# First sums behind the retention multiplied later, and a third gate tile ahead of the first latent projection

## The chip, the cores and the metric

The kernel runs on one core of one Trainium2 chip. The time is the device time of one execution in microseconds; lower is better. Three runs of the kernel before took 850.65, 853.06 and 853.61 us, median 853.06 us.

## What is computed

Three blocks in a row on x of 256 positions by 1024 channels, all in fp32. The change lies in the first two:

```python
# layer 0, retention: its tail
y = (silu(gate) * group_norm(o)) @ w_out          # 2048 -> 1024
x = x + rms_norm(y, post_norm_g)                  # needs the sum of y*y over the channels
x = x + (p @ ple_w_proj) * sigmoid(x @ ple_w_gate)
# layer 1, latent attention: 16 heads
z = rms_norm(x) @ w_in                            # c_q 768, c_kv 256, k_rope 64, gate 2048
c_q, c_kv = rms_norm(z[:768]), rms_norm(z[768:1024])
q = c_q @ w_uq;  k = c_kv @ w_uk;  v = c_kv @ w_uv
o = softmax(causal(q k^T + q_rope k_rope^T)) v
y = (silu(gate) * o) @ w_out
```

The third block is a convolution block with a feed-forward part, which the change does not touch.

## The kernel before

Channels lie on the partitions, so a tile of a projection is 128 output channels by 256 positions. Every operand is split into a high and a low part, and one product is three matmuls (lines 237 to 239): high by high, high by low, low by high. A call of `mm` does these three. Weights come in loads of 128 by 1024 (eight tiles) through SP's queue; a load is cast to its high part on ScalarE (L178) and subtracted to its low part on VectorE (L179), into five buffers each. Activations are split in the same way by L187 (ScalarE) and L188 (VectorE).

The order of the work is written out by hand with a clock that counts only planned TensorE time: each call of `mm` moves it on by 3 x 256 / 2400 = 0.32 us, and `after(us, fn)` puts `fn` at the first call that ends at or past the due time. On top of that the Tile framework puts the instructions of each engine into a list: earlier in the program goes first, but what its own estimate takes as not ready is passed by what is. The engines then work through their lists in that order.

**The tail of the retention.** `out_proj` runs the output projection: eight blocks m of 128 channels, for each the last four of sixteen input blocks (four calls, twelve matmuls). When the block pairs (0,1), (2,3), (4,5) end, `done` gives them to `Sums.feed`: squares on ScalarE (L327) and their running sum on VectorE (L331). Blocks 6 and 7 come singly. `Sums.flush` takes a PSUM bank, starts the reciprocal root's function on ScalarE with one element (`warm`, L317) and multiplies the running sum by a matrix of ones (L341, two fp32 matmuls, each shown as two); `Sums.end` squares a single block (L357) and adds its product with ones. `flush` falls due 1.0 after block 5, the end of block 6 falls due 1.28 after block 6, and `done(7)` ends the rest. Then `post` takes the reciprocal root, scales and adds (L379 to L381, L367 to L373, L690, L691), splits, and runs the gate projection `ple_gate0`; between them stands `ple_proj` (tiles php), which needs none of this.

**The latent attention.** After the six tiles of c_q, `lora` falls due 4.0 later: sum, reciprocal root, scaling (L792) and split (L187, L188) of the six tiles `lat` that all of `mla_proj` needs. The loop over p (eight pairs of heads) is quoted by the program below. `mla_gate(n)` is sixteen calls of `mm` into two banks, a scaling on VectorE (L831) and a Silu on ScalarE (L832). `mla_proj(p)` is 26 calls: 6 for the rotary part of q, 12 for the rest of q, 4 for k, 4 for v; rotary part and splits follow on ScalarE (L756, L187, copies) and VectorE (L758 to L760, L188). `mla_scores(p)` falls due 3.07 after a projection; it is followed by the softmax (VectorE L896 to L909, ScalarE exponentials L901 and L902), 7.6 later by `mla_turn` (transposes, L920, and splits) and 2.59 after that by `mla_av`. With the list `[2, 4, 6, 8, ...]` two gate tiles stand ahead of each of the first four projections and none ahead of the last four. A step of the modulation for the third block (L413, `ada`, with a DMA) is put in every 7.61 of the planned clock.

Of the kernel before, what the change touches and what calls it, by code (L numbers as in the profile page):

```python
# [82 lines left out]
def tile_kernel(ctx, tc, order, xT, pT, pos, vec, cst, cv, rows, wada, wts, outT):  # L83
# [56 lines left out]
    def small(n):  # L140
        return sp.tile([P, n], F32, tag="small", name=nm("sm"), bufs=8)
# [61 lines left out]
    def after(us, fn):  # L203
        queue.append((clk[0] + us, fn))
        queue.sort(key=lambda e: e[0])
# [4 lines left out]
    def mod_rate(us):  # L210
        mods["rate"], mods["last"] = us, clk[0]
# [13 lines left out]
    def drain():  # L225
        busy[0] = True
        while queue:
            due, fn = queue.pop(0)
            clk[0] = max(clk[0], due)
            fn()  # L230
        busy[0] = False
# [425 lines left out]
    def proj_sums(both, get, key):  # L657

        sums = Sums(both, 0)

        def done(m, ys):
            x = get(m, ys)
            if m < 6:
                sums.feed(x)
                if m == 5:
                    after({"r": 1.0, "m": 0.96}[key], sums.flush)
            elif m == 6:
                after({"r": 1.28, "m": 1.06}[key], lambda: sums.end(x, False))
            else:
                drain()  # L670
                sums.end(x, True)
        return sums, done
# [66 lines left out]
    sums, done = proj_sums(False, lambda m, ys: ys.piece(m), "r")  # L739
# [82 lines left out]
    def mla_gate(p):  # L822

        if p % 2 == 0:
            sgs[p // 2] = Blk(4)
        ps = bank2()
        for b in range(2):
            for kb in range(8):
                mm(ps[:, b, :], seq_g.next(), rhs(xp, kb), kb == 0, kb == 7)
        gr = t2()  # L830
        V.scalar_tensor_tensor(gr, ps, -0.5, bc2(r1["nr"]), MUL, MUL)  # L831
        A.activation(sgs[p // 2].pair(p % 2), gr, AF.Silu)  # L832
# [12 lines left out]
    def mla_proj(p):  # L845
        st = hd[p]
        psr = bank()[:, :S]
        for kb in range(6):
            mm(psr, seq_q.next(), lat_rhs(kb), kb == 0, kb == 5)
        qr = st["qr"] = (t1(F32R, "qrh", 2), t1(F32R, "qrl", 2))  # L850
        rope4(psr, lambda a: split(qr[0], qr[1], a))
        psq = bank2()
        for b in range(2):
            for kb in range(6):
                mm(psq[:, b, :], seq_q.next(), lat_rhs(kb), kb == 0, kb == 5)

        qk0 = st["qk0"] = t2().rearrange("p x (b t) -> p x b t", b=2)
        qp = t2(F32R).rearrange("p x (b t) -> p x b t", b=2)
        qn = st["qn"] = [qp[:, i] for i in range(2)]
        split(*qn, psq[:, :, P:])  # L860
        A.copy(qk0[:, 0], psq[:, :, :P])
        psk = bank2()
        for b in range(2):
            for kb in range(2):
                mm(psk[:, b, :], seq_k.next(), lat_rhs(kb, 6), kb == 0, kb == 1)
        kn = st["kn"] = (t2(F32R), t2(F32R))
        split(kn[0], kn[1], psk)
        A.copy(qk0[:, 1], psk[:, :, :P])
        psv = bank2()
        ws = [seq_v.next() for _ in range(2)]  # L870
        for b in range(2):
            bs = slice(b * P, (b + 1) * P)
            for kb in range(2):
                c = lat_rhs(kb, 6)
                mm(psv[:, b, :], (c[0][:, bs], c[1][:, bs]), ws[kb], kb == 0, kb == 1)
        v = st["v"] = t2(F32R), t1()
        split(v[0][:, 0, :], v[0][:, 1, :], psv[:, 0, :])
        A.copy(v[1], psv[:, 1, :])

    def mla_scores(p):  # L880
        st = hd[p]
        qn, kn, qr, qk0 = st["qn"], st["kn"], st["qr"], st["qk0"]
        st["p"] = []

        ps0 = bank()[:, :S].rearrange("p (e t) -> p e t", e=2)
        mm(ps0, (qr[0][:, :P], qr[1][:, :P]), (kr[0][:, :, :P], kr[1][:, :, :P]), True, False)
        ps1 = bank2()
        mm(ps1, (qr[0][:, P:], qr[1][:, P:]), kr, True, False)
        for e in range(2):
            mm32(ps0[:, e, :], qk0[:, 0, e, :], qk0[:, 1, e, :], False, e == 1)  # L890
        for e in range(2):
            mm(ps1[:, e, :], (qn[0][:, e, :], qn[1][:, e, :]), (kn[0][:, e, :], kn[1][:, e, :]), False, e == 1)
        for e in range(2):
            sm = tp.tile([P, 384], F32, tag="am", name=nm("sm"), bufs=2)
            mx = small(2)
            V.tensor_tensor_reduce(sm[:, :P], ps0[:, e, :], causal[:, P:], 1.0, NEG, ADD, ALU.max, mx[:, 0:1])  # L896
            V.tensor_tensor_reduce(sm[:, P:], ps1[:, e, :], causal, 1.0, NEG, ADD, ALU.max, mx[:, 1:2])
            ngm = small(2)
            V.tensor_scalar(ngm, mx, -1.0, None, MUL)
            ssum = small(2)  # L900
            A.activation(sm[:, :P], sm[:, :P], AF.Exp, bias=ngm[:, 0:1], accum_out=ssum[:, 0:1])  # L901
            A.activation(sm[:, P:], sm[:, P:], AF.Exp, bias=ngm[:, 1:2], accum_out=ssum[:, 1:2])  # L902
            rin = small(2)
            V.reciprocal(rin, ssum)
            for i, part in enumerate((sm[:, :P], sm[:, P:])):
                if 0 >> (2 * (p > 3) + i) & 1:
                    A.activation(part, part, AF.Copy, scale=rin[:, i:i + 1])
                else:
                    V.tensor_scalar(part, part, rin[:, i:i + 1], None, MUL)  # L909
            st["p"].append(sm)  # L910
        after(7.6, lambda: mla_turn(p))
# [30 lines left out]
    mod_rate(7.61)  # L942
    ng = 0
    for p in range(8):
        while ng < [2, 4, 6, 8, 8, 8, 8, 8][p]:
            mla_gate(ng)
            ng += 1
        if p == 4:
            mod_rate(12.84)
        mla_proj(p)  # L950
        after(3.07, lambda p=p: mla_scores(p))

    sums, done = proj_sums(False, lambda m, ys: ys.piece(m), "m")
# [446 lines left out]
    for tb in range(2):  # L1400
# [19 lines left out]
        sq, r = small(1), small(1)  # L1420
# [86 lines left out]
```

## Time and profile before

| | |
|---|---|
| median of 3 runs | 853.06 us (850.65 to 853.61) |
| the profiled execution | 847.85 us, of which the span of instructions is 846.1 us |
| TensorE (PE) busy | 826.1 us, 98% of the span, 6114 matmuls |
| VectorE (DVE) busy | 703.1 us, 83% |
| ScalarE (ACT) busy | 555.2 us, 66% |
| granted TensorE clock | 0.997 of full speed, mean |

Busy times overlap. A matmul of 256 columns is shown with some 0.28 us, but a new one starts about every 0.12 us, so PE's busy time is the time in which at least one is under way. In the rows, the time in square brackets is the idle time of the engine just before an instruction, and behind the arrow stands what ended it.

### The profile page before, as it was taken

What the parts mean: (1) busy time and instruction counts of PE and PEld (TensorE: products, weight loads), DVE (VectorE), ACT (ScalarE), POOL (GpSimd) and SP (SyncE); (2) the same over time, 40 slices, a digit from 0 to 9 for tenths busy, and PEclk for the clock granted to TensorE, in tenths of its full rate; (3) what the DMA queues carried; (4) which work ended last, traced back from release to release, by engine and by line L of the source; (5) the groups of instructions that cost most, each with busy time, mean ns of one, the idle gap of its engine ahead of it and who ended that gap; (6) DMA issues with size and microseconds to landing.
All of it is one profiled execution on the core that took longest, in us unless ns stands there. A gap on an engine that the chain in (4) does not pass through costs nothing.

```text
span 846.1 us, 15771 instructions
## 1 busy us (share of the span) xinstructions
PE 826.1 (98%) x6114; PEld 787.9 (93%) x6114; DVE 703.1 (83%) x1283; ACT 555.2 (66%) x968; POOL 9.9 (1%) x30
## 2 busy tenths in 40 slices
PE   8999999999999999998999999999999999999995
PEld 6989999999999989998999999999998999999885
DVE  6999798988889978688874768899677888889986
ACT  7655565545676686777754857999756576666550
POOL 0000000000000000000000000000000000000001
PEclk9999999999999999999999999999999999999998
DMA  9875567778556637374255364245463455567722
GB/s 335 323 258 212 215 217 269 255 264 319 171 182 248 223 145 259 116 263 145 99 184 176 121 224 152 98 150 199 148 224 128 134 190 191 184 214 255 277 77 75
DMA packets 46634, 167.48 MB, mean 198 GB/s; under 512 B 5216, under 2 KB 5472, under 8 KB 46560
## 3 DMA queue, kind: packets, MB, share of 16 engines
q1 hardware_dynamic: 45936, 164.38, 55.1%
q0 software_dynamic: 624, 2.10, 0.9%
q8 instruction: 48, 0.79, 0.4%
q14 instruction: 26, 0.21, 0.1%
HBM read 165.41 MB, written 1.05 MB: 197 GB/s over the span
## 4 chain that ended last, share of the span: by engine, by line
PE 50%; DVE 2%; ACT 1%; issue 1%; DVEq 0%
PE ps L238 13%; PE ps L237 13%; PE ps L239 13%; PE ps L243 10%; PE ps L341 1%; PE ps L363 0%; DVE wl L179 0%; PE ps L920 0%; PE ps L1170 0%; DVE t L1434 0%; DVE sm L1415 0%; DVE half L690 0%; DVE t L1411 0%; DVE t L1412 0%; PE ps L1407 0%
## 5 line engine op out<-in xcount | busy, mean ns | idle before, releaser
L237 PE MATMUL ps<-half,wh 128*128 128x256 f32 x1504 | 425.4, 284 | 1.4 <-ACT half L187 1.4
L238 PE MATMUL ps<-half,wh 128*128 128x256 f32 x1504 | 423.8, 282 | 0.6 <-DVE half L188 0.5
L239 PE MATMUL ps<-half,wl 128*128 128x256 f32 x1504 | 422.0, 281 | 1.1 <-DVE wl L179 1.0
L178 ACT CAST wh<-raw 128x1024 fp32r<-128x1024 f32 x233 | 243.5, 1049 | 154.9 <-PE ps L238 94.8
L179 DVE TENSOR_TENSOR wl<-raw,wh 128x1024 fp32r<-128x1024 f32 x233 | 282.7, 1219 | 59.5 <-ACT wh L178 57.3
L239 PEld LDWEIGHTS ps<-half,wl 128*128 128x128 f32 x1504 | 283.8, 189 | 1.7 <-DVE wl L179 1.7
L238 PEld LDWEIGHTS ps<-half,wh 128*128 128x128 f32 x1504 | 283.4, 188 | 1.9 <-DVE half L188 1.0
L237 PEld LDWEIGHTS ps<-half,wh 128*128 128x128 f32 x1504 | 282.5, 188 | 2.6 <-ACT half L187 2.0
L243 PE MATMUL ps<-half,raw 128*128 128x256 f32 (+2 forms) x384 | 84.9, 380 | 0.0
L243 PEld LDWEIGHTS ps<-half,raw 128*128 128x128 f32 x384 | 72.5, 190 | 10.0
L237 PE MATMUL ps<-wh,half 128*128 128x512 f32 (+1 forms) x202 | 72.6, 360 | 0.9 <-ACT wh L178 0.9
L413 DVE CUSTOM_DVE_ANT_0 adach<-adach,siluc 128x1024 f32<-128x1024 f32 x48 | 58.4, 1218 | 16.7 <-DMA adach<-in_wada 16.7
L238 PE MATMUL ps<-wl,half 128*128 128x512 f32 (+1 forms) x202 | 71.0, 351 | 0.5 <-DVE wl L179 0.5
L239 PE MATMUL ps<-wh,half 128*128 128x512 f32 (+1 forms) x202 | 71.0, 352 | 0.0
L1087 ACT ACTIVATE t<-apad,vec 128x256 f32<-128x256 f32 x106 | 44.3, 501 | 0.5 <-DVE half L1088 0.5
L237 PEld LDWEIGHTS ps<-wh,half 128*128 128x128 f32 x202 | 37.9, 188 | 6.8 <-ACT wh L178 1.7
L238 PEld LDWEIGHTS ps<-wl,half 128*128 128x128 f32 x202 | 38.1, 189 | 6.0 <-DVE wl L179 1.0
L239 PEld LDWEIGHTS ps<-wh,half 128*128 128x128 f32 x202 | 38.0, 188 | 5.6
L1088 DVE TENSOR_TENSOR half<-half,t 128x512 f32<-128x512 f32 x53 | 36.5, 689 | 3.7 <-ACT t L1087 1.8
L187 ACT CAST half<-t 128x256 fp32r<-128x256 f32 (+1 forms) x47 | 20.3, 453 | 17.9 <-DVE t L1347 10.9
L188 DVE TENSOR_TENSOR half<-t,half 128x256 fp32r<-128x256 f32 (+1 forms) x47 | 21.7, 482 | 4.5 <-ACT half L187 3.6
L1342 ACT ACTIVATE t<-ps,vec 128x256 f32<-128x256 f32 x38 | 21.0, 558 | 2.0 <-PE ps L239 1.2
(290 smaller groups left out, 908.1 us busy)
## 6 DMA issues: line engine op xcount, KB each, us to landing
raw<-in_wts SPq DMA_DIRECT2D x257, 512.0 KB, 4.1
adach<-in_wada SPq DMA_DIRECT2D x48, 512.0 KB, 5.0
half<-in_xT SPq DMA_DIRECT2D x4, 256.0 KB, 5.7
half<-in_rows POOLq DMA_DIRECT2D x2, 512.0 KB, 4.7
out<-t SPq DMA_DIRECT2D x4, 256.0 KB, 2.0
cst<-in_cst SPq DMA_DIRECT2D x1, 928.0 KB, 10.6
raw<-in_wts SPq DMA_DIRECT2D x2, 256.0 KB, 4.4
siluc<-in_cv SPq DMA_DIRECT2D x1, 512.0 KB, 9.0
```

What stands on the lines that cost most here:

```text
L178: A.copy(hi, raw)
L179: V.tensor_sub(lo, raw, hi.bitcast(F32))
L187: A.copy(hi, src)
L188: V.tensor_sub(lo, src, hi.bitcast(F32))
L237: T.matmul(ps, l[0], r[0], start=first, stop=False)
L238: T.matmul(ps, l[0], r[1], start=False, stop=False)
L239: T.matmul(ps, l[1], r[0], start=False, stop=last)
L243: T.matmul(ps, w, r, start=first, stop=last)
L413: V.tensor_tensor_reduce(ch, ch, sc, 1.0, 0.0, MUL, ADD, mod[:, n:n + 1])
L1087: A.activation(t[:, b, :], apad[:, i0 + b, k:k + S], AF.Copy, scale=w[b])
L1088: V.tensor_add(acc.pair(i0 // 2), acc.pair(i0 // 2), t)
L1342: A.activation(t[:, b, :], ps[:, b, :], AF.Identity, bias=col("b_dw_f_2", m), scale=w[2])
```

## The change

Two numbers. The first sums behind the retention fall due 2.0 instead of 1.0 of the planned clock after block 5. The list of gate tiles begins with 3 instead of 2: gate tile 2 is called ahead of `mla_proj(0)` and not behind it, so that one tile (3) instead of two stands between the first and the second projection. All else is as it was; nothing is computed more or less.

```diff
@@ proj_sums, done
                 if m == 5:
-                    after({"r": 1.0, "m": 0.96}[key], sums.flush)
+                    after({"r": 2.0, "m": 0.96}[key], sums.flush)
@@ the loop over the pairs of heads
     for p in range(8):
-        while ng < [2, 4, 6, 8, 8, 8, 8, 8][p]:
+        while ng < [3, 4, 6, 8, 8, 8, 8, 8][p]:
             mla_gate(ng)
             ng += 1
```

## Rows read from the trace of the kernel before

**Rows 1.** The page, part 1: busy us, share of the span, instructions of each engine.

```profile
PE 826.1 (98%) x6114; PEld 787.9 (93%) x6114; DVE 703.1 (83%) x1283; ACT 555.2 (66%) x968; POOL 9.9 (1%) x30
```

**Rows 2.** Windows: stretch, length; busy us (instructions) of PE, PEld, DVE, ACT, POOL; clock; DMA.

```profile
207.00:218.00 11.00, 9.65 (x72) 9.06 (x72) 9.20 (x18) 7.96 (x17) 0.00 (x0) 1.00 0.61 207
264.00:280.20 16.20, 14.83 (x125) 14.57 (x124) 15.53 (x29) 8.28 (x12) 0.00 (x0) 1.00 0.73 259
280.20:293.10 12.90, 12.90 (x108) 12.90 (x109) 12.09 (x25) 9.89 (x20) 0.00 (x0) 1.00 0.55 192
293.10:312.00 18.90, 17.47 (x140) 16.60 (x139) 13.82 (x33) 16.10 (x30) 0.00 (x0) 1.00 0.38 138
...
363.00:390.00 27.00, 25.95 (x213) 25.28 (x213) 22.78 (x59) 19.98 (x44) 0.20 (x1) 1.00 0.61 210
390.00:404.00 14.00, 12.25 (x101) 11.95 (x101) 12.91 (x34) 11.18 (x33) 0.00 (x0) 1.00 0.47 164
```

**Rows 3.** Timelines of ACT, DVE and PE at the tail of the retention: start, length, instruction.

```profile
207.18 0.38 ACT L357 ACTIVATE t<-ps 128x256 f32<-128x256 f32 x1
...
207.41 1.22 DVE L179 TENSOR_TENSOR wl<-raw,wh 128x1024 fp32r<-128x1024 f32 x1
208.55 0.68 DVE L331 TENSOR_TENSOR t<-t,t 128x512 f32<-128x512 f32 x1
...
209.37 1.53 PE L341 MATMUL ps<-t,ones 128*128 128x256 f32 x6 [1.09 <-DVE t L331]
...
217.58 0.39 PE L238 MATMUL ps<-half,wh 128*128 128x256 f32 x1 [0.26 <-DVE half L188]
```

**Rows 4.** Timeline of PE where the first latent projection begins.

```profile
280.19 0.62 PE L237 MATMUL ps<-half,wh 128*128 128x256 f32 x3 [1.37 <-ACT half L187]
```

**Rows 5.** Timeline of DVE around the same place.

```profile
277.67 1.22 DVE L179 TENSOR_TENSOR wl<-raw,wh 128x1024 fp32r<-128x1024 f32 x1
278.80 1.65 DVE L792 SCALAR_TENSOR_TENSOR t<-ps,gq,t 128x256 f32<-128x256 f32 x4
280.37 1.42 DVE L188 TENSOR_TENSOR half<-t,half 128x256 fp32r<-128x256 f32 x4
...
283.09 1.22 DVE L179 TENSOR_TENSOR wl<-raw,wh 128x1024 fp32r<-128x1024 f32 x1
284.23 0.75 DVE L188 TENSOR_TENSOR half<-t,half 128x256 fp32r<-128x256 f32 x2
```

**Rows 6.** Timeline of PE from the first scores to the second projection.

```profile
294.15 0.61 PE L243 MATMUL ps<-t 128*128 128x128 f32 x4
...
303.38 0.70 PE L920 MATMUL ps<-ident,sm 128*128 128x128 f32 x3 [0.45 <-DVE sm L909]
...
305.06 0.39 PE L239 MATMUL ps<-half,wl 128*128 128x256 f32 x1 [0.73 <-DVE wl L179]
...
308.40 0.39 PE L239 MATMUL ps<-half,wl 128*128 128x256 f32 x1 [0.24 <-DVE wl L179]
```

**Rows 7.** Timeline of ACT in the same stretch, and its first Silu table.

```profile
281.08 1.28 ACT L832 ACT_TABLE_LOAD   x1
...
298.59 1.28 ACT L832 ACT_TABLE_LOAD   x1
299.89 0.63 ACT L832 ACTIVATE half<-t 128x512 f32<-128x512 f32 x1
300.52 1.28 ACT L901 ACT_TABLE_LOAD   x1
301.82 0.41 ACT L901 ACTIVATE sm<-sm,sm 128x128 f32<-128x128 f32 x1
...
304.51 1.49 ACT L756 COPY t<-ps 32x256 f32<-32x256 f32 x4
```

**Rows 8.** The page, part 5: the cast that splits activations (mean ns of one).

```profile
L187 ACT CAST half<-t 128x256 fp32r<-128x256 f32 (+1 forms) x47 | 20.3, 453 | 17.9 <-DVE t L1347 10.9
```

## The prediction

> **What bounds the kernel.** I read the page first: PE is under way for 98% of the span [rows 1]. A change that adds and removes no matmul can win only what PE stands idle, so the next view is the windows over the two places that are edited [rows 2]. The reader subtracts PE's busy time from the length of each stretch: 1.35 us of idle time at the tail of the retention (207 to 218), 1.37 where the first latent projection begins (264 to 280.2), none while that projection runs (280.2 to 293.1), 1.43 from the first scores to the second projection's start (293.1 to 312), then 1.05 and 1.75 around the pairs of heads that have no gate tile ahead of them (363 to 404). The granted clock is 1.00 in all of these stretches, the full 2.4 GHz, so no idle time here lowers it. Then the timelines say what ended each idle time [rows 3, 4, 6] and what VectorE and ScalarE did meanwhile [rows 3, 5, 7]. From the stretch without idle time comes the pace: 12.90 us over 108 matmuls is 0.119 us a matmul, 0.36 us a call of three, 5.7 us a gate tile of sixteen calls [rows 2].
>
> **Part 1, the first sums.** By the planned clock the sums were called after the fourth call of block 6 (4 x 0.32 = 1.28, past 1.0); with 2.0 they are called after the third call of block 7 (7 x 0.32 = 2.24). That is three calls later, 9 x 0.119 = 1.07 us of PE's work. But on PE they did not stand where they were called. Block 6 was ready by 207.18, when its square starts; PE went on with matmuls until 209.37 - 1.09 = 208.28, and the next thing it did was to wait 1.09 us for the running sum, which VectorE had begun only at 208.55, behind a weight subtraction of 1.22 us [rows 3]. So the framework had already put block 7 ahead of the sums, and the new place in the program, still ahead of block 7's last call, gives it no reason to put them elsewhere. What of `flush` moves is one bank, one activation of one element and two fp32 matmuls; SP's and POOL's queues are not passed, no DMA moves. The end of block 6 falls due at 1.28 + 1.28 = 2.56, behind 2.24, so the order of the three sums stays.
>
> Even if they did move, it would not pay. The sums stand on a chain: running sum, sums, reciprocal root, scaling, split, gate projection, and at its end PE waits again, 0.26 us at 217.58 [rows 3]. Work of `ple_proj` put ahead of the sums fills the 1.09 and makes the chain that much later, so the idle time turns up at 217.58. The chain is not shorter by anything in the diff. I take 0. Bounds: -1.1 if the chain should have slack that I do not see, +0.5 if the two matmuls, 4 of the 6 shown in 1.53 us, that is 1.0 us, come half behind other work and push the chain.
>
> **Part 2, the third gate tile.** PE ends gate tile 1 at 280.19 - 1.37 = 278.82 and waits for the first split part of `lat` [rows 4]. VectorE is the reason: from 277.67 to 284.98 (284.23 + 0.75) its rows follow each other without a gap worth naming, scaling and splitting the six tiles with two weight subtractions between [rows 5]; it was busy 15.53 of the 16.20 us up to 280.2 [rows 2]. With the change PE begins gate tile 2 at 278.82 and works on it until 278.82 + 5.7 = 284.5. The last of `lat` is there at 284.98, and the projection wants its fifth input block only 4 x 0.36 = 1.4 us after its start, at 285.9. So the 1.37 us goes and nothing comes in its place, if the gate tile itself does not wait. It needs x (long there) and two weight loads. After 280.19 PE used up its first load in 8 x 0.36 = 2.9 us, and went on into the second at 283.1 without idle time [rows 2], though the subtraction of 283.09 was only then starting [rows 5]: VectorE is at least two loads ahead, and the next two loads in the queue are the gate's instead of the projection's, at the same points of the program. SP's queue thus carries the same transfers in another order: the two loads of gate tile 2 ahead of the projection's five, not behind. Its scaling (L831) and Silu also come earlier by a projection. Value: -1.37 us; bounds -1.6 (the first calls behind the wait are issued out of order, for which I allow 0.2) and -0.7 (half of it spent on a late weight subtraction).
>
> Then the other side. What was behind the projection is now ahead of it: between the first scores and the second head's transposes PE had gate tiles 2 and 3 to work on, now the last six calls of gate tile 3 and the second projection. The call of the transposes lies 7.6 / 0.32 = 24 calls behind the scores in either case, some 8.6 us by the measured pace; in the trace the transposes of the second head came 303.38 - (294.15 + 0.61) = 8.6 us after the fp32 part of the scores, with 0.45 us of waiting [rows 6]. The cover is thus as long as before in calls, but other work now competes on VectorE and ScalarE: rotary copies and splits of the second projection instead of a gate tile's scaling and Silu. Against that stands ScalarE's function table: a Silu with its table sits between the two heads' exponentials, 298.59 to 301.82, which is 3.2 us by which the second head is later [rows 7]. A gate tile still ends six calls behind the first scores (tile 3 in place of tile 2), so this stays; but one Silu on its own goes (tile 2 joins tiles 0 and 1 behind the load at 281.08), and with it two loads of 1.28 us. The stretch had 1.42 us of waits on PE (0.45 + 0.73 + 0.24) [rows 6]. The nearest rows: the pairs without a gate tile ahead had 1.05 and 1.75 [rows 2]. Bounds: -1.42 (all gone) and 1.05 + 1.75 - 1.42 = +1.4; with one gate tile left it lies between, and I take 0, the row of this very place.
>
> ScalarE's table is where the Trainium skill would give another size: "ScalarE: Activation LUTs", section What ACT_TABLE_LOAD costs, states about 1.28 us for the load and 1.38 us of draining, 2.66 us a switch. Here the exponential starts 301.82 - 300.52 = 1.30 us after its load starts [rows 7], so the load's part agrees and no drain of that size shows. By the page two switches fewer would free 5.3 us of ScalarE, by the rows 2.6; neither is on PE's path, and the sum stays.
>
> **The sum.** Profiled execution 847.85 us, of it 846.1 span: 0 - 1.37 + 0 = -1.37 us, which gives 846.5. That execution is 5.2 us quicker than the median of the runs, which scatter by 3 us; the difference does not depend on that, so the median goes from 853.06 to 851.7 us, or -0.16%.
>
> **Rivals.** First, *the cover is also better*: with two table loads fewer and the gate's scaling out of the way, the 1.42 us goes too. -1.37 - 1.42 = -2.8, 850.3 us. For it: 1.28 us loads in the chain of the second head [rows 7], and two of the three waits there are for a weight subtraction that VectorE did late. Against it: the Silu between the heads stays.
>
> Second, *a new wait, slower than before*: the second projection's ScalarE work stands in front of the second head's exponentials and of the splits of the transposed heads. Four copies take 1.49 us [rows 7], two casts some 0.45 each [rows 8], together 2.4; six more copies and casts up to the values, at the same 0.45, are 2.7 in front of the transposes' splits. If all 5.1 were in PE's way the time would be +3.7 (856.8); half of it, which I take as its price because the cover is not used up on all of it, is 2.55 - 1.37 = +1.2, 854.2 us. It decides the sign once the waits between the scores and the end of `mla_av(0)` exceed 1.42 + 1.37 = 2.8 us. For it: 12.91 of 14.00 us of VectorE and 1.75 us of idle PE where no gate tile is left [rows 2]. Against: ScalarE's 16.10 of 18.90 us here [rows 2] hold table loads, of which two go. This rival is what a rule of the Trainium skill speaks for ("TensorE: Matmul & The Clock Gate", section Architectural detail: ScalarE's and VectorE's queues are strictly first in, first out): an exponential that is ready can't pass a copy that waits. The chance of this rival stays as the rows give it.
>
> Third, *it does not do what it says*: the framework had already filled or would again spend the 1.37 us, as a late weight subtraction ahead of gate tile 2. Then 853.1 us.
>
> **How the numbers follow.** Forecast (front gap gone, the rest as it was) 0.55; also the second gap gone 0.17; a new wait 0.17; nothing 0.11. The range reaches from the first rival with a lower bound of part 1 and 2 on top (850.3, less up to 1.3) to the second at its price: 849.0 to 854.4. That leaves out the fully exposed rival and the scatter of medians beyond. About 0.5%, 4.3 us, is what a measurement can tell from no change here. All idle time of PE in the edited stretches is 1.35 + 1.37 + 1.43 = 4.2 us, so faster by more needs all of it: 0.05. Slower by more needs more than the full second rival (+3.7): 0.04. Within: 0.91.
>
> **What would show it.** Right: the timeline of PE goes from gate tile to gate tile to projection without the 1.37 us, the sums of ones still stand behind all of block 7 with about 1.1 us of wait, one Silu table and one exponential table fewer, three waits of about 1.4 us in total between scores and second projection. Wrong: a wait for VectorE's low weights inside gate tile 2; transposes that wait over 1 us for the softmax; sums of ones among block 7's matmuls or behind those of `ple_proj`.

## The result, and the profile after

The changed kernel took 843.24 us (842.56 to 844.22, 4 runs) beside 853.12 us (850.65 to 853.61, 4 runs) of the kernel before: ratio 0.9891, 95% interval 0.9869 to 0.9913. I had forecast 851.7 in a range down to 849.0. In two later sessions the gain was smaller, but still many times the forecast one: 0.9919 (0.9900 to 0.9938) for the gate tile alone and 0.9927 (0.9902 to 0.9952) for the changed kernel again. So some 6.5 to 10 us went, where I had seen 1.4.

The page of after, part 1 (beside [rows 1]), and its windows (stretch, length, busy us of PE, PEld, DVE, ACT, POOL, granted clock, DMA share, GB/s; beside [rows 2], with the same work in each and one more stretch, 310 to 333, which I had not read of before):

```profile
PE 823.7 (98%) x6114; PEld 787.2 (94%) x6114; DVE 702.4 (84%) x1283; ACT 552.7 (66%) x966; POOL 9.9 (1%) x30
```

```profile
205.70:216.70 11.00, 10.41 (x79) 9.82 (x79) 9.20 (x18) 8.78 (x19) 0.00 (x0) 1.00 0.62 204
262.70:278.90 16.20, 16.20 (x138) 16.14 (x136) 14.98 (x28) 8.24 (x11) 0.00 (x0) 1.00 0.70 254
278.90:297.50 18.60, 18.60 (x157) 18.47 (x156) 17.75 (x33) 15.13 (x27) 0.00 (x0) 1.00 0.65 227
297.50:310.00 12.50, 11.54 (x98) 11.28 (x97) 7.99 (x27) 10.37 (x22) 0.00 (x0) 1.00 0.25 93
310.00:333.00 23.00, 23.00 (x194) 22.87 (x194) 20.98 (x43) 16.06 (x35) 0.00 (x0) 1.00 0.75 270
358.00:385.00 27.00, 26.20 (x216) 25.52 (x215) 23.03 (x59) 20.09 (x45) 0.20 (x1) 1.00 0.60 211
385.00:399.00 14.00, 12.23 (x101) 11.93 (x101) 12.84 (x35) 11.17 (x32) 0.00 (x0) 1.00 0.47 163
```

The idle time in front of the first projection is gone (16.20 of 16.20). From there to 333 us one wait is left, 0.96 us, in the place of the three of [rows 6]. The two pairs without a gate tile wait nearly as they did (0.80 and 1.77 us idle, 1.05 and 1.75 before). The timelines of PE, at the sums (beside [rows 3]) and over all of 262 to 333 us:

```profile
208.04 1.53 PE L341 MATMUL ps<-t,ones 128*128 128x256 f32 x6 [0.23 <-DVE t L331]
...
306.59 0.30 PE L920 MATMUL ps<-ident,sm 128*128 128x128 f32 x1 [0.96 <-DVE sm L909]
```

ScalarE of after (beside [rows 7]): three Silus share the first table; one Silu with its table still stands between the exponentials of the two heads. Two loads fewer: 966 instructions, not 968.

```profile
280.18 1.28 ACT L832 ACT_TABLE_LOAD   x1
...
285.04 0.62 ACT L832 ACTIVATE half<-t 128x512 f32<-128x512 f32 x1
...
299.94 1.28 ACT L832 ACT_TABLE_LOAD   x1
301.24 0.63 ACT L832 ACTIVATE half<-t 128x512 f32<-128x512 f32 x1
303.64 1.28 ACT L901 ACT_TABLE_LOAD   x1
```

**Where the time went in the two profiled executions.** I matched the matmuls of the two traces by their count along PE and compared their starts (counted from the first instruction of an engine, 0.12 us less than in the rows). The 1901st, the last that I took from the common part of the two programs, started at 259.43 and 258.11: -1.32 us ahead of every edit that matters. From there to the end it is 586.50 and 582.54 us: -3.96, made of -1.67 at the front of the first projection, -1.0 from the first scores to the second projection, -0.78 at the transposes of the second pair, -0.29 near 386 us and -0.2 elsewhere. Those are -5.3 us together; the medians differ by more. Three questions follow: which of the two parts did it, what are the 1.32 us, and what do the medians hold that this pair of traces does not?

### The profile page after: what moved, and what is told of

Read it like the earlier page. It is cut to its first block, busy times and chain, and to the rows that moved or that the text cites. A ratio compares the mean times of both kernels' runs of the same rounds, so it can differ in the third digit from the quotient of the medians.

```text
span 840.8 us, 15768 instructions
## 1 busy us (share of the span) xinstructions
PE 823.7 (98%) x6114; PEld 787.2 (94%) x6114; DVE 702.4 (84%) x1283; ACT 552.7 (66%) x966; POOL 9.9 (1%) x30
## 3 DMA queue, kind: packets, MB, share of 16 engines
HBM read 165.41 MB, written 1.05 MB: 198 GB/s over the span
## 4 chain that ended last, share of the span: by engine, by line
PE 51%; DVE 2%; ACT 1%; issue 1%; DVEq 0%
PE ps L238 13%; PE ps L237 13%; PE ps L239 13%; PE ps L243 10%; PE ps L341 1%; PE ps L363 0%; DVE wl L179 0%; PE ps L920 0%; PE ps L1170 0%; DVE t L1434 0%; DVE sm L1415 0%; DVE half L690 0%; DVE t L1411 0%; DVE t L1412 0%; PE ps L1407 0%
## 5 line engine op out<-in xcount | busy, mean ns | idle before, releaser
L413 DVE CUSTOM_DVE_ANT_0 adach<-adach,siluc 128x1024 f32<-128x1024 f32 x48 | 58.6, 1222 | 13.8 <-DMA adach<-in_wada 13.8
```

What stands on the lines that cost most here:

```text
L413: V.tensor_tensor_reduce(ch, ch, sc, 1.0, 0.0, MUL, ADD, mod[:, n:n + 1])
```

## The experiments

The kernel before ran beside each of them, in six sessions, 11 to 25 times in each, with medians of 850.3 to 851.6 us. The ratios are those on record with each run; they can differ from the quotient of the two medians by up to 0.14%. "Lost to the clock" below is the span times (1 - mean granted clock) of an execution. In each of the twenty traces 1.7 to 3.3 us of it lie behind the last matmul, where the clock is 0.50 and PE has nothing left to do; only what goes beyond that costs time.

**Each part alone.**

```diff
 e1_sums_only:  after({"r": 2.0, "m": 0.96}[key], sums.flush)   # gate tiles as before
 e2_gate_only:  while ng < [3, 4, 6, 8, 8, 8, 8, 8][p]:          # sums as before
```

> Only the first edit (2.0 instead of 1.0); gate list as before. In the lists of every engine this differs from the kernel before in the name of one PSUM bank and one small tile alone, so it is also a second look at the kernel before. Theory A (the whole gain comes from the gate tile): ratio 1.000, within 0.2%; the 1.1 us wait ahead of the sums varies with when transfers land, here anything from 0.2 to 1.1. Rival B (the sums give 1 us or more of the gain): ratio 0.998 or below.

> Only the second edit (gate list 3, 4, 6, 8); the sums as before. Theory A: the whole gain, ratio 0.989 as the full change, 843 us; the timeline of PE goes from gate tile 2 into the first projection without the 1.37 us wait. Rival B: a part of the gain is missing, ratio 0.991 or above. Rival C (the runs of before that gave 853 us were made under other conditions than those of after): the ratio comes nearer to what the two profiled spans show, 840.8 to 846.1, that is 0.994.

The sums alone: 849.38 us, ratio 0.9991 (0.9969 to 1.0012). The compiled program has the same list of instructions and waits on every engine as before; only the names of two buffers differ. So this gives a second trace of the kernel before, and it shows how the same program varies:

```profile
210.80 1.53 PE L341 MATMUL ps<-t,ones 128*128 128x256 f32 x6 [1.07 <-DVE t L331]
...
281.95 0.62 PE L237 MATMUL ps<-half,wh 128*128 128x256 f32 x3 [1.72 <-ACT half L187]
283.02 0.39 PE L238 MATMUL ps<-half,wh 128*128 128x256 f32 x1 [0.22 <-DVE half L188]
```

The gate tile alone: 843.49 us, ratio 0.9919 (0.9900 to 0.9938), and 582.57 us from the 1901st matmul to the end (582.54 with both parts). It is the whole change.

**Other numbers of gate tiles.** Four ahead of the first projection; three and five; one more ahead of each pair.

```diff
 e3_four_ahead:      [4, 4, 6, 8, 8, 8, 8, 8]
 e4_five_by_second:  [3, 5, 6, 8, 8, 8, 8, 8]
 e10_one_each:       [3, 4, 5, 6, 7, 8, 8, 8]
```

> Gate list 4, 4, 6, 8: all the first four gate tiles ahead of the first projection and none between the first and the second. If the gain is the front wait alone, this keeps it and loses the cover of the first softmax: 1 to 3 us slower than the full change, ratio about 0.991 to 0.993. If the gain comes from Silu tables and competition in the first softmax, one more Silu leaves it and the time stays or falls by another 0.5 to 1 us, ratio 0.988.

> Gate list 3, 5, 6, 8: the third tile ahead of the first projection as in the change, but two tiles between first and second projection and one between second and third. If only the front wait matters, the time is that of the full change, ratio 0.989. If the place of the single tile decides, the waits move from the stretch before the second projection to the stretch before the third, and the time differs by up to 1 us either way.

> Gate tiles finished ahead of the eight projections: 3, 4, 5, 6, 7, 8, 8, 8 (the changed kernel: 3, 4, 6, 8, 8, ...). Theory (one gate tile ahead of a pair covers its softmax, none leaves 0.7 to 1.8 us): the front and the first softmax stay as in the changed kernel, the waits 0.68 at 385 and 1.77 at 396 go or fall under 0.5 each: 1.5 to 2.5 us less than the changed kernel, 841 to 842 us. Rival (each single tile brings its Silu and two table loads, 2.6 us of ScalarE, between two heads): waits of 0.5 to 1.7 at the transposes of every pair, 843 to 846.

All three have the third tile ahead of the first projection, and none waits there. Still they took 846.01 (0.9951, 0.9934 to 0.9968), 848.86 (0.9984, 0.9968 to 1.0000) and 849.59 us (0.9973, 0.9950 to 0.9996): most of the gain can be lost again behind the front (in e3 the transposes at 314.64 us wait 1.68 us for a weight cast on ScalarE). In e4 a wait of 1.92 us for a low weight half stands at 308 us. VectorE's timeline names its origin, a modulation step that stood ahead of the softmax's next instruction and of the weight subtraction, and waited for its own DMA:

```profile
305.66 1.22 DVE L413 CUSTOM_DVE_ANT_0 adach<-adach,siluc 128x1024 f32<-128x1024 f32 x1 [2.68 <-DMA adach<-in_wada]
...
306.88 1.22 DVE L179 TENSOR_TENSOR wl<-raw,wh 128x1024 fp32r<-128x1024 f32 x1
```

In e10 it is ScalarE: two single Silus, each with a load of its own and one for the exponential that follows, stand among one pair's exponentials, and PE's transposes wait 3.32 us. Timelines of PE and of ScalarE there, the second of the two Silus' pairs of loads:

```profile
392.17 0.30 PE L920 MATMUL ps<-ident,sm 128*128 128x128 f32 x1 [3.32 <-DVE sm L909]
```

```profile
387.28 1.28 ACT L832 ACT_TABLE_LOAD   x1
...
389.22 1.28 ACT L901 ACT_TABLE_LOAD   x1
```

**The modulation steps moved a little, in the order of before.** New theory: what makes PE wait is VectorE's list, in which the steps (L413) stand among work that PE needs. Two runs put the next steps back by 15.6 us of the planned clock, from the first (e5) or the second (e6) pair's projection on. In the changed order, e11 does the latter.

```diff
         mla_proj(p)
+        if p == 0:                  # e5_front_relieved; p == 1: e6, e11
+            mods["last"] += 15.6
```

> The kernel before, gate tiles 2, 4, 6, 8; only the pace of the modulation steps is put back by 15.6 us when the first head pair's projection has been written, so that the two steps that VectorE executed at 276.18 and 284.90 (1.22 us each, and the wait for their DMA) are made up later, in the output projection. No computation is left out. Theory (the wait of PE in front of the first projection is VectorE's backlog): one step fewer ahead of the splits of the latent makes the 1.37 us shorter by up to 1.3, the waits of the first softmax (0.45, 0.73, 0.24) stay, ratio to before 0.997 to 0.9985. Rival (the wait is set by the statistics of the latent on ScalarE, and VectorE's backlog is not the last to come): 1.37 stays, ratio 1.000. Clock theory (the wait of 1.4 us is what brings the half clock in some executions): ratio under 0.997 and a mean granted clock of 0.997 or more in the median execution. The wait at the sums behind the retention, in a program that is the same up to there: 1.1 us if it belongs to the program, 0.2 to 1.1 if it is chance.

> The kernel before, only with the modulation steps put back by 15.6 us when the second head pair's projection has been written: the step that VectorE executed at 295.77, behind a wait of 0.67 for its DMA, between the first scores and the second head's transposes, and the one behind it, are made up later. No computation is left out. Theory (work that stands in VectorE's list between the softmax's instructions makes PE's waits there): the waits 0.45, 0.73, 0.24 fall by 0.7 to 1.4 us in sum, the 1.37 ahead of the first projection stays; ratio 0.9975 to 0.999. Rival (ScalarE's tables between the two heads set them): no change, ratio 1.000.

> The changed kernel with the modulation steps put back by 15.6 us when the second pair's projection has been written, so that no step that waits for its DMA stands between the first scores and the second head's transposes on VectorE. No computation is left out. Theory (VectorE's list makes the last wait of 0.96 at the second head's transposes): it goes, 0.7 to 1.3 us less than the changed kernel, 842 to 842.8 us. Rival (the wait is ScalarE's, by the table between the two heads): 0.96 stays, 843.3, no change.

e5: 846.59 us (846.24 to 847.21), ratio 0.9955 (0.9942 to 0.9968). Two steps less, and the wait in front of the first projection falls from 1.37 to 0.24; the waits behind it grow (1.44 and 0.73). So VectorE's list sets the front's wait, as the theory had it. The total is more than the 1.3 us of it, and the profiled execution doesn't show where: it took 586.50 us from the 1901st matmul to the end, as before, with a stretch at half the clock behind the wait of 0.73. e6: 849.03 us, ratio 0.9980 (0.9962 to 0.9997), with 0.16 and 0.76 of the three softmax waits left and none at the second pair's transposes. e11: the wait of 0.96 is gone as expected, and from the 1901st matmul to the end it is 581.95 us, 0.6 less than in after; its median of 844.96 us (0.9907, 0.9887 to 0.9927) can't be told from the changed kernel's.

**ScalarE's table left out.** Both kernels leave out the Silu of the latent attention's gates.

```diff
-        A.activation(sgs[p // 2].pair(p % 2), gr, AF.Silu)
+        A.activation(sgs[p // 2].pair(p % 2), gr, AF.Copy)   # e7 from before, e8 from after
```

> The kernel before with the Silu of the latent-attention gate tiles left out (a plain copy in its place, 0.68 us as the Silu), so that ScalarE's function table is not changed for them; nothing else differs, and the order of all work is that of before. What is left out is the Silu of these gates. Theory (a Silu with its table between the two heads' exponentials, 3.2 us, makes the second head late): the waits 0.45, 0.73 and 0.24 go, 1.2 to 2.0 us with the restart of PE, the 1.37 ahead of the first projection stays; ratio 0.9975 to 0.9985. Rival (VectorE's list sets them): ratio 1.000 and the waits as before.

> The changed kernel with the same Silu of the latent-attention gates left out in the same way. Theory (what the change won in the first softmax is one table change fewer; one is left between the two heads): the last wait, 0.96 us at the second head's transposes, goes: 0.8 to 1.3 us less than the changed kernel, 842.0 to 842.6, ratio to before 0.990; against the kernel before with one table it is then better by the front alone, 1.4 to 1.9 us. Rival (the change's gain in the softmax is the order of VectorE's work): 0.96 stays, 843.3, and it stays better than the kernel before with one table by 3 us or more.

e7: 846.63 us, ratio 0.9953 (0.9934 to 0.9972); the three softmax waits are gone, so the table between the heads was a cause of them in the order of before, beside the step that e6 moved. e8: 843.67 us (0.9918, 0.9899 to 0.9937), nothing gained on the changed kernel: the 0.96 became 0.72, and 1.81 came for a low weight half. e7 also shows what sets the front. VectorE ran the same instructions as in [rows 5], but the step ahead of them waited 1.37 us for its DMA (in before it did not wait), and PE's wait was 2.35 us instead of 1.37. In the four traces of this order in which the step waits and nothing fills the gap, PE's wait in front of the projection is the step's wait plus 0.97 to 1.00 us: 1.53 for 0.53 (e12), 1.71 for 0.71 (e6), 1.72 for 0.75 (e1), 2.35 for 1.37 (e7). In the changed order the same step waits 0.55 (after), 0.84 (e15) and 1.27 us (e2), and PE, with the gate tile to work on, doesn't wait. VectorE and PE of e7:

```profile
276.76 1.23 DVE L413 CUSTOM_DVE_ANT_0 adach<-adach,siluc 128x1024 f32<-128x1024 f32 x1 [1.37 <-DMA adach<-in_wada]
...
279.39 1.66 DVE L792 SCALAR_TENSOR_TENSOR t<-ps,gq,t 128x256 f32<-128x256 f32 x4
```

```profile
280.36 0.62 PE L237 MATMUL ps<-half,wh 128*128 128x256 f32 x3 [2.35 <-ACT half L187]
```

**The wait filled, not shortened.** Twelve useless matmuls stand ahead of the first projection, in the bank that it overwrites. The lists of the other engines are those of before, so the latent comes no earlier. A third trace of the kernel before (e12) was taken with it.

```diff
         psr = bank()[:, :S]
+        [T.matmul(psr, xp[1][kb][:, :P], xp[0][kb], start=True, stop=True)
+         for kb in [0, 1, 2, 3, 4, 5, 6, 7, 0, 1, 2, 3] if p == 0]
```

> The kernel before with 12 useless matmuls (x times x, 128x256, into the bank that the first projection then overwrites) right ahead of the first latent projection; the lists of all other engines are those of before. At the pace of before, 0.117 to 0.119 us each, they are 1.40 to 1.43 us and fill the wait of 1.37 us, while the latent comes no earlier. If a wait costs the time that it is shown: no change (ratio 1.000, at most +0.1 us). If a wait also costs a restart of PE (0.3 us by the alignment of the two traces): -0.3 us, ratio 0.9996. If it also brings stretches at half the clock in some executions: the median granted clock goes from 0.995 to 0.996 or 0.997, the time by 1 to 2.5 us, ratio 0.997 to 0.9988, and the scatter of the runs shrinks.

> The kernel before once more, for a further trace of the same program. If the difference of the two profiled executions ahead of the edited places (1.3 us up to 262 us, in programs that are the same there) is chance, the matmul that stood at 259.43 us comes anywhere between 258.1 and 262.7 here, and from there to the end of the kernel it is 586.4 us again (586.50 and 586.30 in the two traces so far; 582.5 in two traces of the changed order).

e9: 850.23 us, ratio 0.9974 (0.9954 to 0.9993). PE does nothing useful in the time, and the kernel is still quicker. The median lost to the clock goes from 4.24 us (116 executions of before, all sessions) to 2.55; what is left of the span without that loss is 845.2 us in the median of before and 845.3 in that of e9. The time itself is 1.0 us shorter by the medians of the session and 2.2 us by the ratio. The third trace of before, e12, shows the same thing from the other side. PE's timeline, and windows around its waits:

```profile
279.80 0.62 PE L237 MATMUL ps<-half,wh 128*128 128x256 f32 x3 [1.53 <-ACT half L187]
280.87 0.58 PE L238 MATMUL ps<-half,wh 128*128 128x256 f32 x1 [0.22 <-DVE half L188]
...
334.79 0.61 PE L920 MATMUL ps<-ident,sm 128*128 128x128 f32 x3 [2.18 <-DVE sm L909]
```

```profile
276.00:280.00 4.00, 2.46 (x21) 2.27 (x20) 3.80 (x7) 2.14 (x4) 0.00 (x0) 1.00 0.88 297
280.80:284.00 3.20, 3.13 (x14) 3.13 (x15) 3.20 (x8) 3.17 (x6) 0.00 (x0) 0.50 0.31 125
284.20:288.00 3.80, 3.80 (x35) 3.80 (x33) 2.12 (x6) 0.82 (x1) 0.00 (x0) 1.00 0.67 230
...
335.40:338.80 3.40, 3.40 (x18) 3.40 (x18) 3.13 (x5) 2.61 (x7) 0.00 (x0) 0.50 0.71 233
```

Behind each of the two waits the granted clock is 0.50, the lower of its two levels (1.2 GHz), and PE starts 14 matmuls in 3.20 us where it starts 35 in 3.80 afterwards. Fourteen at that later pace are 1.5 us, so 1.7 us are lost in the first of these stretches. The trace of before on which I predicted had no such stretch ahead of its last matmul, and that of e1 had one alone, at 12.4 us, behind waits at the start of the kernel that both orders have. Only 14% of the executions of before have a mean clock of 0.997 or more; of the 16 executions of the changed order (after, e2, e15) 11 have. The mean alone doesn't tell whether an execution had such a stretch: the trace of e2 has 0.996 and none ahead of its last matmul. The Trainium skill ("Perfetto Trace Analysis", section Matmul Optimizations) says that the matmul engine scales its power with its utilisation, so that matmuls should come back to back; by that rule e9 should gain without any useful work, and by its ratio (0.9954 to 0.9993) it does.

**All steps out of the first four pairs.** The steps are held until the loop reaches p = 4, the fifth pair, and made up behind it, from both orders; e15 is the changed kernel again.

```diff
-    mod_rate(7.61)
+    mods["rate"] = None
...
         if p == 4:
-            mod_rate(12.84)
+            mod_rate(6.0)
```

> The kernel before without modulation steps up to the fourth head pair; they are made up behind it at twice the pace (every 6.0 instead of 12.84 us of the planned clock). No computation is left out. Theory (gate tile and steps share the gain): the second pair's wait (0.1 to 2.2 us, 0.8 in the middle of four traces) and its scatter go, the front's wait falls from 1.4 to 1.7 us to about 0.2, as in the run with two steps fewer; about 4 to 5 us less than before, 846 to 847, ratio 0.9945 to 0.996. If the steps were all of it: 843 to 844, as the changed kernel. If they were nothing: ratio 1.000.

> The changed kernel with the modulation steps moved in the same way. Theory (in the changed order the steps are hidden): 842.5 to 844, within 1 us of the changed kernel in the same session, the wait of 0.96 at the first transposes gone or under 0.3. Against e13 it is better by the first softmax and the front that is left, 2 to 3 us. Rival (the gate tile gives nothing beyond the room that the steps took): the same time as e13 within 0.8 us.

> The changed kernel once more, in the same session. By the first comparison 0.9891 (0.9869 to 0.9913), by its part alone on the other chip 0.9919: 0.990 to 0.993 here. From the matmul at 258 us to the end 582.5 us again, if no stretch at half the clock falls into it; ahead of that 258.1 to 262.7.

e13, in the order of before with two gate tiles ahead: 843.61 us, ratio 0.9918 (0.9892 to 0.9944), and 581.16 us from the 1901st matmul to the end, less than in the changed kernel. e14: 845.40 (0.9931, 0.9905 to 0.9957) and 583.07. e15: 845.08 (0.9927, 0.9902 to 0.9952) and 582.78. I had expected e13 to keep half of the loss; the rival "the steps were all of it" gave 843 to 844, and that came. But it came from two places. From the 1901st matmul to the 2521st, behind the transposes of the second pair, before takes 78.94 us, the changed kernel 75.39, e13 75.77 and e14 74.31; from there to the end it is 507.56, 507.14, 505.39 and 508.76 us. So in the stretch that the change edits the gate tile gives 3.55 us, holding back the steps 3.17 and both together 4.63: without the steps the third gate tile still gives 1.46. That e13 is level with the changed kernel comes from 2.17 us at the later pairs, which the change leaves alone (14.00 of 14.00 below; 12.25 in [rows 2] and 12.23 in after); e14 loses 1.2 us there. Why the steps made up later cost e14 time and not e13, no run shows. Windows of e13, then VectorE at the front (16.00 of 16.00: no wait, beside [rows 2, 4, 5]), then PE in the first softmax, where two waits are left that e14 hasn't:

```profile
263.00:279.00 16.00, 16.00 (x136) 15.95 (x135) 13.92 (x26) 9.24 (x13) 0.00 (x0) 1.00 0.63 200
...
292.00:311.00 19.00, 18.07 (x149) 17.58 (x147) 12.72 (x31) 16.10 (x29) 0.00 (x0) 1.00 0.34 112
...
388.00:402.00 14.00, 14.00 (x119) 13.87 (x118) 12.77 (x34) 11.33 (x30) 0.00 (x0) 1.00 0.63 205
```

```profile
275.75 0.42 DVE L789 TENSOR_TENSOR t<-t,t 128x256 f32<-128x256 f32 x1
276.21 1.27 DVE L792 SCALAR_TENSOR_TENSOR t<-ps,gq,t 128x256 f32<-128x256 f32 x3
277.39 0.75 DVE L188 TENSOR_TENSOR half<-t,half 128x256 fp32r<-128x256 f32 x2
```

```profile
301.93 0.39 PE L239 MATMUL ps<-half,wl 128*128 128x256 f32 x1 [0.17 <-DVE wl L179]
...
305.84 0.38 PE L239 MATMUL ps<-half,wl 128*128 128x256 f32 x1 [0.76 <-DVE wl L179]
```

The first two splits start at 277.39 instead of 280.37: the step is 1.3 us of that, and the weight subtraction that stood ahead of the scalings in [rows 5] now follows the splits.

**A better version, tried three times.** In seven of the seventeen traces so far, of either order, PE also waits for a low weight half near 193 us. They are the seven in which the 1901st matmul starts latest, at 261.1 us or later (the others at 260.8 or earlier). e15 shows the same cause; VectorE, then PE:

```profile
190.88 1.23 DVE L413 CUSTOM_DVE_ANT_0 adach<-adach,siluc 128x1024 f32<-128x1024 f32 x1 [0.95 <-DMA adach<-in_wada]
...
192.03 1.22 DVE L179 TENSOR_TENSOR wl<-raw,wh 128x1024 fp32r<-128x1024 f32 x1
```

```profile
193.30 0.39 PE L239 MATMUL ps<-half,wl 128*128 128x256 f32 x1 [1.36 <-DVE wl L179]
```

So e16 to e18 also thin out the steps in the retention's output projection and make up for them later.

```diff
 ys, prep = out_proj("ret_out", ret_g, 12, 4.0, done, 0)   # e16, e17: 1.8 -> 4.0; e18: 2.4
 mod_rate(4.5)      # from p = 4 on; e16 from before, e17 from after; e18 from before: 4.8
```

> The order of before, and modulation steps neither in the head pairs up to the fourth nor in the dense part of the retention's output projection (planned pace 4.0 instead of 1.8 us there; made up from the fourth pair on, every 4.5 us). No computation is left out. Theory (steps that wait for their DMA in VectorE's list make PE's waits at 189 to 194 us too): no wait of PE for low weights between 185 and 200, the matmul that stood at 259.43 us comes at 258.3 or sooner, 1 to 2 us less than with the head pairs alone relieved (843.6): 841.5 to 843. Rival (the weights' own DMAs are late there): the waits appear as before, 843 to 845, and the steps put into the later pairs make them slower by up to 2 us.

> The same in the order of the changed kernel. Theory: 841.5 to 843.5, no better than the same pace of steps in the order of before, since nothing is left for the gate tile to hide. Rival (the gate tile covers something of its own): 1.5 us or more below the run in the order of before.

> The order of before; modulation steps at a planned pace of 2.4 instead of 1.8 us in the retention's output projection, none in the head pairs up to the fourth, every 4.8 us behind it; all are done some 30 us before the latent attention's output projection ends. No computation is left out. Theory (the loss of the kernels with late steps was the debt behind 470 us): no wait of 4 us at 480, the pairs' waits as with the head pairs alone relieved, and fewer or shorter waits at 189 to 194: 842 to 844 us, ratio 0.989 to 0.992, the changed kernel's or a little better. Rival (sixteen steps in the pairs 4 to 7 cost there what they cost ahead): waits of 1 to 2 us at the transposes of those pairs, 845 to 848.

None of the three waits near 193 us any more (ten of the seventeen others don't either), and the 1901st matmul starts at 258.42, 258.55 and 258.35. But e16 (849.29 us, 0.9970, 0.9954 to 0.9987) and e17 (849.58, 0.9984, 0.9969 to 1.0000) pay for it: steps that are left over stand in VectorE's list behind 470 us (in e16 at 473.75, with a wait of 1.00 us for its DMA, and at 476.79) ahead of what PE needs. PE of e16 shows

```profile
481.04 1.01 PE L237 MATMUL ps<-half,wh 128*128 128x256 f32 x3 [4.63 <-ACT half L187]
```

e18 ends its steps before that and has no such wait: 845.45 us (844.93 to 846.84), ratio 0.9940 (0.9918 to 0.9962). It waits 1.02 and 1.82 us at the transposes of later pairs, where before waits 1.75 once and e13 not at all; its rival had that in part. No version measurably better than the changed kernel came of it; e13 equals it in time.

## Why the prediction was wrong

The forecast was the front's wait alone, -1.37 us. It failed where it put three terms at nothing: the first softmax and the pair behind it (-1.0 and -0.78 us in the two traces), the granted clock (-1.7 to -2.6 in the medians), and the difference between the profiled execution and a typical one (some -0.9).

**Part 1: right.** The sums stay where they were, because the program comes out the same. That their wait fell from 1.09 to 0.23 us is chance: it is 1.07 in e1, which has the change, 0.69 in e12, which has not, and 1.03 in e15, which has.

**The front: the right place, a size too small, a row too late.** The wait goes, as forecast. But 1.37 shown were 1.67 us by the starts of the matched matmuls: the idle time in brackets runs from the end of one matmul to the start of the next, but matmuls of 0.28 us overlap and start every 0.12 us, and from start to start it was 1.65 us here, with the next start another 0.1 late. And 1.37 was the mildest of the traces of this order: 1.53 + 0.22 in e12, 1.72 + 0.22 in e1, 1.71 + 0.22 in e6, 2.35 + 0.20 in e7. I gave VectorE as the reason and began my rows at 277.67 [rows 5]; the modulation step a little earlier is what made VectorE late, by its own 1.2 us and by the weight subtraction that falls behind the splits without it (e5, e13). VectorE of before:

```profile
276.18 1.22 DVE L413 CUSTOM_DVE_ANT_0 adach<-adach,siluc 128x1024 f32<-128x1024 f32 x1
```

In this trace the step doesn't wait for its DMA. That it can, and that PE's wait then grows with it, only the other traces show (e1, e6, e7, e12).

**"First-softmax stretch: 0", and no look behind it.** The step that failed is the row "of this very place" taken for what stays. It was -1.0 us, and the second pair, which was not in my windows at all (they stop at 312 and go on at 363), gave another -0.78. The reason is an order that I did not work out: with the gate tile moved, the modulation steps come to stand elsewhere in VectorE's list. Ahead of the change two steps stand in the second pair's softmax: one ahead of the first head's reciprocal (L904) and the second head's maxima, which also waits for its DMA, and one between the second head's negated maxima (L899) and its reciprocal. Each holds all that follows. VectorE of before, and the first of the two steps in e12:

```profile
324.96 1.23 DVE L413 CUSTOM_DVE_ANT_0 adach<-adach,siluc 128x1024 f32<-128x1024 f32 x1 [1.81 <-DMA adach<-in_wada]
...
328.93 0.16 DVE L899 TENSOR_SCALAR sm<-sm 128x2 f32<-128x2 f32 x1
329.00 1.21 DVE L413 CUSTOM_DVE_ANT_0 adach<-adach,siluc 128x1024 f32<-128x1024 f32 x1
...
331.28 0.15 DVE L904 RECIPROCAL sm<-sm 128x2 f32<-128x2 f32 x1
```

```profile
327.86 1.23 DVE L413 CUSTOM_DVE_ANT_0 adach<-adach,siluc 128x1024 f32<-128x1024 f32 x1 [3.44 <-DMA adach<-in_wada]
```

In three traces of this order the first step waits 1.81, 2.36 (e9) and 3.44 us, and PE's transposes of the second head wait 0.55, 1.11 and 2.18: there are 1.25 us of slack, and all beyond them reaches PE. In e1 the step waits 0.66 us (the second one 0.42), and the transposes start only 0.09 late. In the changed order the first step is still there, ahead of the first head's negated maxima, and waits 1.55 us (0.66 in e2, 0.79 in e15), but the second one comes behind both heads, and PE doesn't wait. VectorE of after:

```profile
319.42 1.23 DVE L413 CUSTOM_DVE_ANT_0 adach<-adach,siluc 128x1024 f32<-128x1024 f32 x1 [1.55 <-DMA adach<-in_wada]
...
324.69 0.17 DVE L904 RECIPROCAL sm<-sm 128x2 f32<-128x2 f32 x1
324.89 0.55 DVE L909 TENSOR_SCALAR sm<-sm,sm 128x128 f32<-128x128 f32 x2
...
326.78 1.22 DVE L413 CUSTOM_DVE_ANT_0 adach<-adach,siluc 128x1024 f32<-128x1024 f32 x1
```

In the first softmax a step stands among the first head's maxima ahead of the change (295.77, with a wait of 0.67 us) and among the second head's behind it (302.56, 0.39), and e6, e7 and e11 show that both the steps and ScalarE's table make waits there. The gate tile takes some of the 1.0 us by itself: without any step e13 still waits 0.17 and 0.76 us, and e14 doesn't.

I had quoted the rule for this from the Trainium skill ("TensorE: Matmul & The Clock Gate", section Architectural detail: strictly first in, first out on ScalarE and VectorE), and the rows agree with it. But I applied it to ScalarE's copies and to a new wait, and not to the steps that already stood in VectorE's list.

**"The granted clock is 1.00, so no idle time here lowers it": wrong.** It was 1.00 in that one execution. In others a wait of PE is followed by a stretch at half the clock, which costs some 1.7 us: at the front in e7 and e12, not in e1 and e6. The median lost to the clock is 4.24 us in before and 2.5 in the changed order (1.7 in the first comparison), so a typical execution has about one such stretch less; e9, which filled the front's wait alone, lost 1.7 us less in the median and was 1.0 to 2.2 us quicker.

**"The difference does not depend on that."** I took the profiled execution, 5.2 us quicker than the median, as a picture of the others. The waits that the change removes were short in it, and no stretch at half the clock followed them. Hence also the wrong bound "all idle time in the edited stretches is 4.2 us": the idle time of a typical execution is longer, and costs more than its length.

**The sum, as the runs show it.** From the 1901st matmul to the end -3.96 us; less loss to the clock, -1.7 to -2.6; longer waits in a typical execution of before, at the front about +0.6 and at the second pair about +0.3 above the profiled one (medians of the traces above). That is some 6.5 to 7.5 of the 6.5 to 10 us, an estimate, since it adds one pair of traces and differences of medians. The rest isn't assigned. The 1.32 us ahead of the 1901st matmul are not part of it: it started at 258.19 to 262.70 us in seven traces of the order of before (before, e1, e5, e6, e7, e9, e12), and at 258.11 to 261.84 in seven of the changed order (after, e2, e3, e4, e8, e10, e11), with programs that are the same up to it.

**The rivals.** The first had the right direction and a price of 2.8 us for what was 3.96 in the traces; I gave it 0.17. Its own stretch gave 1.0 us of its 1.42, and 0.96 us of waiting is left there. The other two have nothing for them: PE's waits between the scores and `mla_av(0)` are 0.96 us, far under the 2.8 from which the second decides. e4 loses 1.92 us in this place, but to a modulation step and not to ScalarE's copies.

**What stays open.** That steps in VectorE's list make PE wait is shown at the front by e5 and e13 and by the waits that grow with the step's (e1, e6, e7, e12), and at the second pair by e6 and e13, which don't wait there. How much of the gain is the hiding of the steps and how much the gate tile's own cover is shown by single traces alone: 3.55 us with the steps in place, 1.46 without them. How the 1.0 us of the first softmax splits between steps, table and cover isn't shown. What decides whether a wait lowers the clock I can't say: 1.53 + 0.22 us did in e12, 1.72 + 0.22 did not in e1, and 3.32 us did not in e10.

## What to carry to other kernels

Read what stands in the in-order list of the helping engine just ahead of the work that PE waits for, filler work with its own DMA above all: such a step belongs where nothing that PE needs is queued behind it, and taking it away may do what more cover does. Before pricing a wait, ask how it varies: a wait that ends with a DMA has no fixed size, and one profiled execution that is quicker than the median has probably the short ones. A wait of TensorE costs its shown length, some 0.3 us more by the starts of its matmuls, and in some executions a stretch at half the clock.

## What the runs showed of the hardware

A wait of 1.4 us in TensorE's work costs more than 1.4 us. By the starts of the matmuls it is some 0.25 to 0.3 us more than the idle time shown (1.67 for 1.37, 1.0 for 0.73, 0.78 for 0.55). In part of the executions the granted clock then falls to 0.50: in e12 behind 1.53 + 0.22 us of waiting and behind 2.18, in e7 behind 2.35 + 0.20, in e4 behind 1.92. In e1 (1.72 + 0.22), e6 (1.71 + 0.22) and e10 (3.32) it stayed at 1.00. Filling such a wait with useless matmuls made the kernel 0.26% (0.07 to 0.46%) quicker. After the last matmul of every trace the granted clock falls to 0.50 too, so a mean clock below 1 is no proof of lost time. The wait of one and the same modulation step for its 512 KB DMA went from 0.66 to 3.44 us between executions of one program, and what PE waited followed it (0.53 to 1.37 us of the step's wait at the front, 1.53 to 2.35 us of PE's).
